# The mixer of a hybrid decoder as chains of steps in one list that fixes TensorE's order, with the substitution on GpSimd

## The chip, the core and the metric

The kernel runs on one core of a Trainium2 chip. A core has five engines with queues of their own, each of which works in order: TensorE (PE in the rows; PEld is its weight load), VectorE (DVE), ScalarE (ACT), GpSimd (POOL) and SyncE (SP), which issues the transfers. They wait for each other by semaphores. Matmul results land in PSUM, which GpSimd doesn't reach in this kernel; everything else is in SBUF. The metric is the time of one execution on the device in microseconds (us).

## The reference

256 tokens of width 1024 with 16 learned tokens ahead (272 columns in the kernel) pass two layers. Each layer is a half-weighted SwiGLU, a mixer and a second half-weighted SwiGLU. The mixer projects once and splits the columns among three groups of heads:

```python
def hybrid_mixer(h, ...):
    proj = h @ w_in
    sb_q, sb_k, sb_v, dn_qkv, dn_z, dn_b, dn_a, s5_u = jnp.split(proj, ...)
    o_sb = rmsnorm(stick_breaking_attention(heads(sb_q), heads(sb_k), heads(sb_v)), sb_out_norm)
    o_dn = gated_deltanet(dn_qkv, dn_z, dn_b, dn_a, dn_conv_w, dn_a_log, dn_dt_bias, dn_out_norm)
    o_s5 = rmsnorm(s5_mixer(s5_u, ...), s5_out_norm)
    return jnp.concatenate([o_sb, o_dn, o_s5], axis=-1) @ w_out

# gated_deltanet: qkv = silu(causal conv of 4 taps); q, k = l2norm; beta = sigmoid(b); g = decay
# per chunk of 64: t_inv = inverse of (I + strictly lower (beta k) k^T * decay)
# u = t_inv (beta v), w = t_inv (beta k exp(g)); state is carried from chunk to chunk
# result: rmsnorm(o, out_norm) * silu(z)
# s5_mixer: complex diagonal scan over time, y = gelu(...), then y * sigmoid(y @ w_glu + b_glu)
# stick_breaking: w = exp(log_sigmoid(z) + sum of log_sigmoid(-z) over later keys), out = w v
```

## The kernel before

All activations lie transposed, features on the 128 partitions and the 272 tokens along the columns. Every float32 product of a large weight is made from three matmuls of split halves (`xh`, `xl` and `wh`, `wl`; `mm3`), so that one projection unit of 128 output features takes 8 blocks times 3, or 24 matmuls of 272 columns. For each unit `weights` brings 512 KB into `raw` by SyncE, ScalarE rounds it to `wh`, and VectorE (for some units GpSimd, by `ON_POOL`) subtracts to get `wl`.

A mixer has 18 units of the input projection: six for the convolved q, k, v of DeltaNet (`conv`), four for S5 (`s5u`), two each for z and the stick-breaking q, k and v. Then it has small work:

- `dn_gates`: the gates, the decay matrices `E`, the key norm (`pn`), the products `LT`.
- `dn_inverse`: the inverse of each chunk's triangle. Blocks of 8 by substitution (`TT8`, `t8`, lines L1003 to L1008, on VectorE: seven pairs of a product and a difference of 9 to 63 elements a partition, then one masked copy to blocks of 32 and a transpose by 32), then blocks of 32, 64 and 128 by pairs of products `px`, `py`.
- `dn_rest`: norm of q, the products, then the state from chunk to chunk (`pk`, `pvn`, `pS`, and `pkt`, `pvt2` for the last tokens); `dn_norm` and `dn_out` (`po`, transposes, times z).
- `s5`: input products `pinc`, states by complex rotations and scans on VectorE (`w`, `x`, `s5z`); `s5_outputs` (`pY`, gelu) and `glu` (`pglu`, 48 matmuls).
- `sb`: `scores` (`pz`), `weights` (sums over later keys into the same `pz`, then Exp), `outputs` (`pob`, norm by `pnb`).

After it, `w_out` is applied in parts: `S` (S5's rows), `Y` (the rest). A part is two units at a time, named by their first output block, 4, 6, 0, 2.

A scheduler of the framework sets the order on each engine from the code's order, dependencies, estimated costs and priorities. The code's order is the string `ORD`; the blocks in `high_priority` (`FIRST` 4000 for gates, inverse and rest, `SECOND` 1500 for the S5 output) are drawn ahead. `HORD` orders the steps of `sb`, `ZT` names the PSUM tag of each head's scores (each tag has two buffers). `phase` places the loads of ScalarE's function tables, five in a mixer, and a NoSync order (`order`) keeps functions behind their table.

## Time and profile before

| | us |
|---|---|
| median of 3 runs (lowest to highest) | 1192.27 (1189.04 to 1202.69) |
| the profiled execution, and its span | 1194.31, span 1192.5 |
| mean granted TensorE clock over the span | 0.972 |
| busy: PE | 1154.8 (97%) |
| busy: VectorE | 853.6 (72%) |
| busy: ScalarE | 614.1 (52%) |
| busy: GpSimd | 175.3 (15%) |

The share of busy time is a mean over stages with different limits. The two mixers lie at 232.9 to 384.8 us and 821.0 to 977.9 us of the span, measured from the norm's sum over all features (`pms`) to the second group of `po` transposes. The granted clock is given as a share of 2.4 GHz, so 0.50 is 1.2 GHz. A busy time of TensorE holds overlapping records: a matmul that stands in the pipeline behind another counts, and so does one that goes slowly.

### The profile page before, as it was taken

The page shows a single profiled execution, that of the slowest core. Times are in us where ns is not written, and L with a number is a line of the kernel's source. Part 1 is how long each engine was busy: PE and PEld are TensorE (multiplying, and loading weights), DVE is VectorE, ACT ScalarE, POOL GpSimd, SP SyncE. Part 2 cuts the span into 40 slices and gives each one's busy share as a digit, 9 for nine tenths or more (in the row PEclk, how much of TensorE's full clock was granted, in tenths as well). Part 3 has the DMA queues.
Part 4 walks back from the last instruction along what each step waited for, and adds up shares of the span by engine and source line. Part 5 has one row for each costly group of instructions (what it writes and reads, how often), then busy time and mean ns, then how long its engine had stood idle before and what let it go on. Part 6 is the DMA issues. An engine that isn't in the chain of part 4 may idle for free.

```text
span 1192.5 us, 23762 instructions
## 1 busy us (share of the span) xinstructions
PE 1154.8 (97%) x9544; PEld 1104.5 (93%) x9544; DVE 853.6 (72%) x1648; ACT 614.1 (52%) x981; POOL 175.3 (15%) x210
## 2 busy tenths in 40 slices
PE   8999999999998999999999999999999989999997
PEld 7999999998786999999999999999988969999985
DVE  7999986699636866555579998756994268666644
ACT  6455575564166654444455556645632566555533
POOL 6312100021010111110201112011210001111100
PEclk9999999999789999999999999999997599999999
DMA  5656545543201455555565555455431015666663
GB/s 182 179 175 180 166 135 160 167 125 108 71 19 54 142 175 177 168 176 171 177 187 177 169 173 172 132 175 156 124 112 33 27 45 185 181 188 191 187 191 117
DMA packets 196858, 173.74 MB, mean 146 GB/s; under 512 B 21300, under 2 KB 193004, under 8 KB 196748
## 3 DMA queue, kind: packets, MB, share of 16 engines
q1 hardware_dynamic: 196732, 172.22, 48.2%
q8 instruction: 75, 1.23, 0.4%
q14 instruction: 35, 0.29, 0.1%
q10 hardware_dynamic: 16, 0.00, 0.0%
HBM read 171.15 MB, written 1.05 MB: 144 GB/s over the span
## 4 chain that ended last, share of the span: by engine, by line
PE 84%; DVE 10%; ACT 3%; issue 1%; DMA 1%; SPq 0%; ACTq 0%; DVEq 0%
PE proj L146 17%; PE proj L145 17%; PE proj L144 17%; PE pd L146 5%; PE pd L145 5%; PE pd L144 5%; PE pd L493 5%; DVE wl L139 2%; PE pY L852 1%; DVE qkv L1346 1%; DVE xT L1437 1%; PE pY L850 1%; PE pl L887 1%; PE pm L783 1%; PE pz L1227 1%
## 5 line engine op out<-in xcount | busy, mean ns | idle before, releaser
L144 PE MATMUL proj<-xh,wh 128*128 128x272 f32 (+1 forms) x1840 | 521.1, 289 | 6.3 <-DVE sy L1435 2.8
L145 PE MATMUL proj<-xl,wh 128*128 128x272 f32 (+1 forms) x1840 | 518.4, 287 | 0.2 <-DVE xl L1296 0.2
L146 PE MATMUL proj<-xh,wl 128*128 128x272 f32 (+1 forms) x1840 | 492.8, 290 | 3.3 <-DVE wl L139 3.0
L136 ACT ACTIVATE wh<-raw 128x1024 fp32r<-128x1024 f32 (+1 forms) x324 | 338.2, 1044 | 292.8 <-PE proj L145 99.5
L139 DVE TENSOR_TENSOR wl<-raw,wh 128x1024 fp32r<-128x1024 f32 (+1 forms) x312 | 378.4, 1213 | 146.6 <-PE pd L146 60.9
L144 PEld LDWEIGHTS proj<-xh,wh 128*128 128x128 f32 x1840 | 345.4, 188 | 10.5 <-DVE sy L1435 4.1
L145 PEld LDWEIGHTS proj<-xl,wh 128*128 128x128 f32 x1840 | 345.2, 188 | 3.0 <-issue 1.5
L146 PEld LDWEIGHTS proj<-xh,wl 128*128 128x128 f32 x1840 | 328.8, 187 | 7.2 <-DVE wl L139 5.8
L144 PE MATMUL pd<-hh,wh 128*128 128x272 f32 x528 | 149.6, 288 | 0.0
L145 PE MATMUL pd<-hl,wh 128*128 128x272 f32 x528 | 149.3, 288 | 0.0
L435 POOL TENSOR_TENSOR hl<-h,hh 128x272 fp32r<-128x272 f32 (+1 forms) x88 | 81.1, 924 | 452.9 <-ACT hh L434 452.8
L146 PE MATMUL pd<-hh,wl 128*128 128x272 f32 x528 | 140.8, 288 | 0.2
L144 PEld LDWEIGHTS pd<-hh,wh 128*128 128x128 f32 x528 | 99.2, 188 | 0.2
L145 PEld LDWEIGHTS pd<-hl,wh 128*128 128x128 f32 x528 | 99.3, 188 | 0.1
L146 PEld LDWEIGHTS pd<-hh,wl 128*128 128x128 f32 x528 | 95.1, 188 | 1.0 <-DVE wl L139 0.9
L107 ACT ACTIVATE g<-g 128x272 f32<-128x272 f32 (+2 forms) x92 | 37.6, 415 | 68.9 <-DVE g L429 68.8
L433 DVE TENSOR_TENSOR h<-proj,g 128x272 f32<-128x272 f32 (+1 forms) x88 | 37.7, 433 | 32.9 <-PE proj L146 21.3
L434 ACT ACTIVATE hh<-h 128x272 fp32r<-128x272 f32 (+1 forms) x88 | 36.4, 419 | 47.1 <-DVE h L433 47.1
L429 DVE TENSOR_TENSOR g<-proj,R 128x272 f32<-128x272 f32 (+1 forms) x88 | 37.5, 430 | 17.8 <-PE proj L146 17.6
L139 POOL TENSOR_TENSOR wl<-raw,wh 128x1024 fp32r<-128x1024 f32 x12 | 30.7, 2557 | 110.5 <-ACT th L107 34.9
L431 DVE TENSOR_TENSOR g<-g,R 128x272 f32<-128x272 f32 (+1 forms) x88 | 37.7, 432 | 12.6 <-ACT g L107 12.3
L376 POOL TENSOR_TENSOR acc<-acc,sq 128x272 f32<-128x272 f32 (+1 forms) x20 | 22.7, 1134 | 91.4 <-ACT sq L370 90.5
(490 smaller groups left out, 1310.1 us busy)
## 6 DMA issues: line engine op xcount, KB each, us to landing
raw<-in_ffn_w_gate_dram SPq DMA_DIRECT2D x88, 512.0 KB, 3.6
raw<-in_ffn_w_up_dram SPq DMA_DIRECT2D x88, 512.0 KB, 3.6
raw<-in_ffn_w_down_dram SPq DMA_DIRECT2D x70, 512.0 KB, 3.5
raw<-in_w_in_dram SPq DMA_DIRECT2D x36, 512.0 KB, 4.4
raw<-in_ffn_w_down_dram SPq DMA_DIRECT2D x24, 384.0 KB, 3.0
raw<-in_w_out_dram SPq DMA_DIRECT2D x16, 512.0 KB, 3.5
raw<-in_s_w_glu_dram SPq DMA_DIRECT2D x4, 512.0 KB, 3.4
xin<-in_x_dram SPq DMA_DIRECT2D x4, 256.0 KB, 5.8
```

The lines of the kernel that those rows point to most:

```text
L107: i = self.nc.scalar.activation(out, in_, func, **k)
L136: nc.scalar.activation(h[:, :n], r[:, :n], AF.Copy)
L139: e.tensor_tensor(l[:, :n], r[:, :n], f32(h[:, :n]), op=ALU.subtract)
L144: mm(p, wh, xh, start=first, stop=False)
L145: mm(p, wh, xl, start=False, stop=False)
L146: mm(p, wl, xh, start=False, stop=last)
L429: V.tensor_tensor(g1, pg[j][:, :N], R, op=ALU.mult)
L431: V.tensor_tensor(g1, g1, R, op=ALU.mult)
L433: V.tensor_tensor(h, pu[j][:, :N], g1, op=ALU.mult)
L434: nc.scalar.activation(hh[:, f, :N], h, AF.Copy)
L435: G.tensor_tensor(hl[:, f, :N], h, f32(hh[:, f, :N]), op=ALU.subtract)
L493: PE.matmul(pd[i][e], x[:, f, ts], w[:, 0, e * 512:e * 512 + 512], start=f == 0 and w is h and x is hh, stop=f == NF - 1 and w is lo)
```

## The change

The parts of the mixer become generators, with a `yield` after each step. One string, `MIX`, names the steps of all parts and the projection units in the order in which they are to be issued: C, U, Q, K, V, Z and a number are a projection unit; g, i, r, a and x advance the gates, the inverse, the rest, stick-breaking and the GLU by one step; p, t and y and a number are the input products, states and outputs of one of S5's four groups; l is the SiLU of the convolved q and v; v the transposes of the attention's values; n the load of the table of exp and ln; m S5's norm; o `dn_norm` and `dn_out`; S a part of `w_out`. Then each matmul of TensorE in the mixer is ordered behind the one before it in the list, by a NoSync dependency. The other engines are still ordered by the scheduler; the priorities are gone.

Beside that, the substitution moves from VectorE to GpSimd; ScalarE copies S5's `pinc` out of PSUM, and the states are then made from SBUF with operations of 544 columns in place of some of 272; z gets its SiLU from Tanh (no table of its own), with the gain and a factor 1/2 in `dn_out`'s scale; the SiLU of q and v comes in one step; the key norm comes ahead of the decay matrices; all scores have the PSUM tag `c`; the two rows of `Y` change places.

```diff
-FIRST, SECOND, URGENT, THIRD = 4000, 1500, 0, 0
-SBP = 0
-ORD = "czsrqgbmn"
-WOUT = "SnY"
-OTAG, NTAG, ZT = "d", "c", "cccd"
-HORD = (0, 1, 4, 2, 5, 3, 8, 6, 7, 9)
 SA, SB = 1, 1
-CONV, UORD, ZK = (0, 1, 4, 5), (0, 1, 2, 3), 0
+MIX = "C2 C3 U0 g U1 g g U2 g g g U3 g Q0 p0 p1 Q1 t0 p2 p3 K0 i t1 K1 a a t2 C0 a a i C1 i t3 a a i C4 i a a i C5 l i " \
+      "y0 V0 i y1 V1 i y2 Z0 y3 Z1 v r r r r x r r x r n a r r r r a m S4 S6 o S0 S2"
...
+        for o in range(2):
+            p = self.psum("b", "pinc")
             for b in range(4):
...
+                PE.matmul(p[:, b * NCH:(b + 1) * NCH], self.W1[o][:, 4 * b + r, :], self.U[:, r, b, :], start=True, stop=True)
+            A.copy(self.S[r][:, o], p[:, :T].rearrange("p (b c) -> p b c", b=4))
...
+        w, x = tl("w"), tl("x")
+        V.tensor_tensor(w, z, bc(cs, 1, 2), op=ALU.mult)
+        V.tensor_tensor(x[:, 0], z[:, 1], sn, op=ALU.mult)
+        V.scalar_tensor_tensor(flat(x[:, 1]), flat(z[:, 0]), -1.0, flat(sn), op0=ALU.mult, op1=ALU.mult)
+        V.tensor_tensor(z, w, x, op=ALU.add)
+        for o in range(2):
+            V.tensor_tensor_scan(flat(z[:, o]), flat(dec), flat(z[:, o]), 0.0, op0=ALU.mult, op1=ALU.add)
...
+        w, x = tl("w"), tl("x")
+        V.tensor_tensor(w, z, bc(cs, 1, 2), op=ALU.mult)
+        V.tensor_tensor(x, z, bc(sn, 1, 2), op=ALU.mult)
+        G.memset(z[:, :, :, 0:1], 0.0)
+        V.tensor_tensor(z[:, 0, :, 1:], w[:, 0, :, :-1], x[:, 1, :, :-1], op=ALU.subtract)
+        V.tensor_tensor(z[:, 1, :, 1:], w[:, 1, :, :-1], x[:, 0, :, :-1], op=ALU.add)
...
+        self.kn, kb = tl([P, 2, TP], "kn"), tl([P, 2, TP], "kb")
+        for b in range(2):
+            k, sq = qkv[:, 2 + b, :], self.c288("sq")
+            A.activation(sq, k, AF.Square)
+            p = self.psum("c", "pn")
+            PE.matmul(p[:, :TP], self.bd64, sq, start=True, stop=True)
+            self.rsqrt(sq, p[:, :TP], bias=self.eps)
+            self.newton(sq, p[:, :TP], self.c288("knt"), 1, EPS)
+            V.tensor_tensor(self.kn[:, b, :], k, sq, op=ALU.mult)
+        yield
         self.E = tl([P, 8, P], "E")
...
         TT8, t8 = tl([P, 9, 8], "TT8"), tl([P, 9, 8], "t8")
-        V.tensor_copy(TT8, bc(self.id8, 1, 9))
+        G.tensor_copy(TT8, bc(self.id8, 1, 9))
         for j in range(7):
-            V.tensor_tensor(t8[:, :, j + 1:], Lb[:, :, j + 1:, j], TT8[:, :, j:j + 1].to_broadcast([P, 9, 7 - j]), op=ALU.mult)
-            V.tensor_tensor(TT8[:, :, j + 1:], TT8[:, :, j + 1:], t8[:, :, j + 1:], op=ALU.subtract)
+            G.tensor_tensor(t8[:, :, j + 1:], Lb[:, :, j + 1:, j], TT8[:, :, j:j + 1].to_broadcast([P, 9, 7 - j]), op=ALU.mult)
+            G.tensor_tensor(TT8[:, :, j + 1:], TT8[:, :, j + 1:], t8[:, :, j + 1:], op=ALU.subtract)
         TT32, T32 = t9("TT32"), t9("T32")
-        V.tensor_tensor(TT32.rearrange("p u (b i) -> p u b i", b=4), bc(TT8, 2, 4),
+        G.tensor_tensor(TT32.rearrange("p u (b i) -> p u b i", b=4), bc(TT8, 2, 4),
                         bc(self.m8c.rearrange("p (b i) -> p b i", b=4), 1, 9), op=ALU.mult)
         V.transpose(fl(T32), fl(TT32))
+        yield
         for k in range(2):
...
         def scores(h):
             hs, b = slice(64 * (h % 2), 64 * (h % 2) + 64), h // 2
-            pz = self.psum(ZT[h], "pz")
+            pz = psum("pz")
             PE.matmul(pz[:, 0:272], k[hs, b, 0:128], q[hs, b, 0:272], start=True, stop=False, **skip)
             PE.matmul(pz[:, 272:416], k[hs, b, 128:256], q[hs, b, 128:272], start=False, stop=True, **skip)
             for c0, n in ((0, P), (272, P), (416, 16)):
...
             A.activation(h, y, AF.Copy)
             V.tensor_tensor(self.xl[:, slot + b, :], y, f32(h), op=ALU.subtract)
-        for x in HORD:
-            (scores if x < 4 else weights if x < 8 else outputs)(x % 4)
+        for f, x in ((scores, 0), (scores, 1), (weights, 0), (scores, 2), (weights, 1), (scores, 3),
+                     (weights, 2), (weights, 3), (outputs, 0), (outputs, 1)):
+            f(x)
+            yield
...
+            def do_z(b):
+                proj(1536, zr, b)
+                t = self.cv("zt")[:, :T]
+                self.act(t, zr[:, b, :], AF.Tanh, scale=0.5)
+                V.scalar_tensor_tensor(zr[:, b, :], t, 1.0, zr[:, b, :], op0=ALU.add, op1=ALU.mult)
+            def silu():
                 self.phase(SET_SILU)
-                for b in range(2):
-                    self.act(zr[:, b, :], zr[:, b, :], AF.Silu)
-                    V.tensor_scalar(zr[:, b, :], zr[:, b, :], self.dng[:, l], None, op0=ALU.mult)
-            def do_s5():
...
-            for x in WOUT:
-                if x == "n":
-                    with first():
-                        self.dn_out(zr, 2)
-                    continue
-                if x == WOUT[-1]:
-                    self.norm_begin(*nxt)
-                for d0 in (4, 6, 0, 2):
-                    w_out_part(x, d0, "ab"[d0 // 2 % 2])
-                    if x == WOUT[-1]:
-                        for d in {4: (4, 5), 6: (6, 7), 0: (), 2: (0, 1, 2, 3)}[d0]:
-                            self.norm_block(d, d0 == 2, t0)
...
+            chains = dict(g=self.dn_gates(l, qkv, ba), i=self.dn_inverse(), r=self.dn_rest(qkv),
+                          a=self.sb(l, q, k, v, 0), x=self.glu(l, u))
+            steps = dict(C=conv, U=s5_in, Q=lambda b: proj(0, q, b), K=lambda b: proj(256, k, b), V=lambda b: proj(512, v, b),
+                         Z=do_z, p=lambda r: self.s5_inputs(u, r), t=self.s5_states, y=lambda r: self.s5_outputs(u, r),
+                         l=silu, v=lambda: self.sb_values(), n=norms, S=lambda d0: w_out_part("S", d0, "ab"[d0 // 2 % 2]),
+                         o=lambda: (self.dn_norm(), self.dn_out(zr, self.dng[:, l], 2)),
+                         m=lambda: self.rms(self.acc, 4 * 512, 0, self.R5, "b"))
+            done = len(nc.cur_bb.bb.instructions)
+            for x in MIX.split():
+                if x in chains:
+                    next(chains[x], None)
+                else:
+                    steps[x[0]](*(int(n) for n in x[1:]))
+            assert all(next(c, 0) == 0 for c in chains.values())
+            pe = [i for i in nc.cur_bb.bb.instructions[done:] if i.engine == mybir.EngineType.PE]
+            for i, j in zip(pe, pe[1:]):
+                self.order(j, i)
+            self.norm_begin(*nxt)
+            for d0 in (4, 6, 0, 2):
+                w_out_part("Y", d0, "ab"[d0 // 2 % 2])
+                for d in {4: (4, 5), 6: (6, 7), 0: (), 2: (0, 1, 2, 3)}[d0]:
+                    self.norm_block(d, d0 == 2, t0)
             self.blocks = (4, 0)
```

Three places show how the order moves. The first is TensorE's queue in layer 0 at the key norm, where `pn` sums the squares `sq` of one block of k. Before:

```order
1733 L144 MATMUL proj<-xh,wh 128x272
1734 L959 MATMUL pn<-sq,bd_384 128x288
1735 L963 MATMUL pbeta<-ba,sel_575 128x288
1736 L145 MATMUL proj<-xl,wh 128x272
1737 L146 MATMUL proj<-xh,wl 128x272 x2
...
1755 L145 MATMUL proj<-xl,wh 128x272
1756 L959 MATMUL pn<-sq,bd_384 128x288
1757 L146 MATMUL proj<-xh,wl 128x272
```

After:

```order
1681 L143 MATMUL proj<-xh,wl 128x272
1682 L926 MATMUL pn<-sq,bd_385 128x288 x2
1683 L939 LDWEIGHTS identb
1684 L939 MATMUL pdc<-negl,identb 128x512
1685 L941 MATMUL pdc<-triI,gs 128x128 x4
1686 L141 MATMUL proj<-xh,wh 128x272
```

Before, the two `pn` stand twenty rows apart, with projections and other products between them; after, they stand side by side ahead of the decay matrix `pdc`.

The second is VectorE's queue in layer 0 at the substitution, the operations on `t` and `TT` (`s5z` are S5's states). Before:

```order
483 L1005 TENSOR_TENSOR t_3313<-Lb,TT_3312 128x9x7
484 L835 TENSOR_TENSOR w<-s5z_3954,cs 128x544
485 L836 TENSOR_TENSOR x<-s5z_3954,sn 128x544
486 L1006 TENSOR_TENSOR TT_3312<-TT_3312,t_3313 128x9x7
487 L1364 SCALAR_TENSOR_TENSOR pq<-proj,R 128x272
488 L139 TENSOR_TENSOR wl<-raw,wh 128x1024
489 L838 TENSOR_TENSOR s5z_3954<-w,x 128x4x67
490 L839 TENSOR_TENSOR s5z_3954<-w,x 128x4x67
491 L1005 TENSOR_TENSOR t_3313<-Lb,TT_3312 128x9x6
492 L825 TENSOR_TENSOR w<-pinc,cs 128x272
```

After, where `T` is the transpose that ends the substitution, and `L1260` belongs to the stick-breaking weights:

```order
476 L824 TENSOR_TENSOR w<-s5z_3458,cs 128x544
477 L825 TENSOR_TENSOR x<-s5z_3458,sn 128x272
478 L826 SCALAR_TENSOR_TENSOR x<-s5z_3458,sn 128x272
479 L827 TENSOR_TENSOR s5z_3458<-w,x 128x544
480 L1387 SCALAR_TENSOR_TENSOR pk<-proj,R 128x272
481 L136 TENSOR_TENSOR wl<-raw,wh 128x1024
482 L829 SCALAR_TENSOR_TENSOR s5z_3458<-dec,s5z_3458 128x272 x2
483 L832 TENSOR_TENSOR w<-s5z_3458,cs 128x544
484 L833 TENSOR_TENSOR x<-s5z_3458,sn 128x544
485 L1260 SCALAR_TENSOR_TENSOR W_588<-pz,W_588 128x432
486 L1014 STREAM_TRANSPOSE T_3644<-TT_3643 128x288
487 L1260 SCALAR_TENSOR_TENSOR W_588<-pz,W_588 128x432
```

And GpSimd's queue after, ahead of that transpose:

```order
47 L136 TENSOR_TENSOR wl<-raw,wh 128x1024
48 L834 MEMSET s5z_3457 128x8
49 L1009 TENSOR_TENSOR t_3627<-Lb,TT_3626 128x9x7
50 L1010 TENSOR_TENSOR TT_3626<-TT_3626,t_3627 128x9x7
51 L1009 TENSOR_TENSOR t_3627<-Lb,TT_3626 128x9x6
```

The pairs of the substitution stood between the operations of the S5 states in one queue; now GpSimd makes them, and VectorE's transpose has its place behind those of the third state.

The third is TensorE's queue in layer 0 at the first norm of the attention's output. Before:

```order
2286 L1251 MATMUL pob<-W_586 64x272
2287 L1252 MATMUL pob<-W_586,W_587 64x144
2288 L1253 MATMUL pob<-W_586,vt 64x16
2289 L1242 MATMUL pz<-W_587,nsufI 128x432
2290 L1243 MATMUL pz<-W_587,nones 128x144
2291 L1244 MATMUL pz<-W_587,nones 128x2x16
2292 L1257 MATMUL pnb<-sbr,bd_384 128x272
```

After:

```order
2229 L1275 MATMUL pob<-W_587 64x272
2230 L1276 MATMUL pob<-W_587,W_588 64x144
2231 L1277 MATMUL pob<-W_587,vt 64x16
2232 L1281 MATMUL pnb<-sbr,bd_385 128x272
2233 L1159 MATMUL pS<-qkv,kg 64x64 x4
2234 L1161 MATMUL pS<-qkv,E 128x64 x4
2235 L1176 MATMUL pkt<-qkv,kn 32x64
```

And ScalarE's queue after, up to the square `sbr` that `pnb` reads:

```order
271 L104 ACTIVATE th<-pglu,prm 128x272
272 L1323 ACTIVATE xh<-s5u,prm 128x272 x3
273 L1328 ACTIVATE gsq<-s5u 128x272
274 L133 ACTIVATE wh<-raw 128x1024
275 L104 ACTIVATE th<-pglu,prm 128x272
276 L94 ACT_TABLE_LOAD
277 L1155 COPY qkv<-pvn 128x256
278 L1323 ACTIVATE xh<-s5u,prm 128x272
279 L1328 ACTIVATE gsq<-s5u 128x272
280 L1279 ACTIVATE sbr<-pob 128x272
```

Before, three matmuls of another head's weights stand between `pob` and `pnb`; after, `pnb` follows `pob` at once and the state's update `pS` stands behind it, while ScalarE has the GLU's operations, a weight and a table load ahead of `sbr`.

## Rows read from the trace of the kernel before

**Rows 1.** Windows: us, length, busy PE, PEld, DVE, ACT, POOL, then clock, DMA share, GB/s.

```profile
232.90:304.80 71.90, 70.02 (x549) 65.96 (x547) 68.23 (x140) 39.28 (x65) 13.03 (x12) 1.00 0.41 118
304.80:324.60 19.80, 17.43 (x284) 14.12 (x288) 12.37 (x27) 2.19 (x5) 0.11 (x1) 0.57 0.18 55
...
341.70:348.50 6.80, 5.96 (x31) 5.77 (x30) 1.92 (x5) 2.85 (x9) 0.73 (x1) 0.50 0.00 0
348.50:384.80 36.30, 32.31 (x248) 25.60 (x247) 22.55 (x51) 25.39 (x51) 3.05 (x2) 1.00 0.19 59
...
500.00:600.00 100.00, 100.00 (x801) 100.00 (x800) 55.86 (x68) 46.24 (x62) 14.13 (x15) 1.00 0.57 174
821.00:892.90 71.90, 70.03 (x550) 65.99 (x548) 68.26 (x140) 39.32 (x65) 13.02 (x12) 1.00 0.41 118
892.90:911.70 18.80, 16.34 (x314) 12.81 (x318) 11.98 (x27) 2.55 (x6) 0.11 (x1) 0.64 0.19 58
...
925.40:949.30 23.90, 23.47 (x120) 22.30 (x119) 4.91 (x15) 9.72 (x23) 2.35 (x1) 0.50 0.07 23
949.30:977.90 28.60, 24.66 (x188) 18.89 (x187) 18.16 (x42) 20.65 (x41) 0.29 (x1) 1.00 0.17 56
```

**Rows 2.** Windows of the tile `proj` alone: length, busy PE, PEld, DVE, then clock.

```profile
232.90:304.80 71.90, 57.93 (x409) 52.79 (x407) 8.50 (x18) 1.00 0.41 118
```

**Rows 3.** ScalarE's groups by form, 232.9 to 384.8: count, busy us, mean ns, idle.

```profile
L136 ACT ACTIVATE wh<-raw 128x1024 fp32r<-128x1024 f32 x22 | 23.2, 1056 | 24.9 <-PE proj L145 24.7
L97 ACT ACT_TABLE_LOAD x5 | 6.4, 1283 | 0.1
...
L107 ACT ACTIVATE W<-W 128x432 f32<-128x432 f32 x8 | 4.2, 556 | 0.0
L107 ACT ACTIVATE W<-pz 128x432 f32<-128x432 f32 x8 | 4.1, 530 | 5.7 <-PE pz L1244 3.4 <-PE pz L1231 2.2
...
L1295 ACT ACTIVATE xh<-s5u,prm 128x272 fp32r<-128x272 f32 x4 | 2.9, 761 | 0.0
L107 ACT ACTIVATE qkv<-qkv 128x272 f32<-128x272 f32 x6 | 2.4, 417 | 1.8 <-DVE qkv L1346 1.8
L1300 ACT ACTIVATE gsq<-s5u 128x272 f32<-128x272 f32 x3 | 2.0, 678 | 0.7 <-DVE s5u L1292 0.7
L107 ACT ACTIVATE th<-pglu,prm 128x272 f32<-128x272 f32 x4 | 1.9, 476 | 0.6 <-PE pglu L146 0.6
```

**Rows 4.** GpSimd's `Lm` group, then timelines at 264 and 286: start, us, operation.

```profile
L1001 POOL TENSOR_TENSOR Lm<-L,lev 128x288 f32<-128x288 f32 x2 | 2.1, 1044 | 6.7 <-ACT qkv L1344 6.7
...
264.24 0.50 DVE L1346 SCALAR_TENSOR_TENSOR qkv<-pad,prm,qkv 128x272 f32<-128x272 f32 x1
...
264.86 1.00 PE L821 MATMUL pinc<-s5U,W 128*128 128x68 f32 x8
264.91 2.37 POOL L139 TENSOR_TENSOR wl<-raw,wh 128x1024 fp32r<-128x1024 f32 x1 [3.25 <-PE proj L146]
265.17 2.95 DVE L1346 SCALAR_TENSOR_TENSOR qkv<-pad,prm,qkv 128x272 f32<-128x272 f32 x2
...
286.55 3.10 POOL L139 TENSOR_TENSOR wl<-raw,wh 128x1024 fp32r<-128x1024 f32 x1 [1.42 <-PE proj L146]
```

**Rows 5.** VectorE's groups by form, 232.9 to 384.8: count, busy us, mean ns, idle.

```profile
L139 DVE TENSOR_TENSOR wl<-raw,wh 128x1024 fp32r<-128x1024 f32 x17 | 20.7, 1216 | 5.5 <-PE proj L146 5.0 <-issue 0.6
...
L832 DVE TENSOR_TENSOR_SCAN s5z<-dec,s5z 128x272 f32<-128x272 f32 x8 | 5.3, 704 | 0.0
...
L835 DVE TENSOR_TENSOR w<-s5z,cs 128x544 f32<-128x544 f32 x4 | 2.9, 718 | 0.0
...
L121 DVE SCALAR_TENSOR_TENSOR sby<-pnb,sbr 128x272 f32<-128x272 f32 x2 | 0.9, 441 | 0.0
```

**Rows 6.** Timeline of one head's scores on TensorE: start, us, first and last form.

```profile
371.60 0.72 PE L1227 MATMUL pz<-pq,pk 64*128 64x272 f32 x2
...
372.73 0.21 PE L1231 MATMUL pz<-pq,pk 64*16 64x16 f32 x2
```

More of the change, by code (lines that the diff above doesn't have):

```diff
@@ new lines, in s5_outputs @@
+    def s5_outputs(self, u, r):
+        PE = self.nc.tensor
+        p = self.psum("b", "pY")
+        for b in range(4):
+            q = 4 * b + r
+            po = p[:, b * NCH:(b + 1) * NCH]
+            PE.matmul(po, self.M0[:, q, :], self.U[:, r, b, :], start=True, stop=False)
+            for k in range(2):
+                PE.matmul(po, self.W2[k][:, q].rearrange("p k g c -> p (k g c)"), self.S[r][:, k, b], start=False, stop=k == 1)
+        for t in range(4):
+            o = u[32 * r:32 * r + 32, :, t * NCH:t * NCH + NCH]
+            self.act(o, p[32 * t:32 * t + 32, :T].rearrange("p (b c) -> p b c", b=4), AF.Gelu_apprx_tanh)
@@ L1183, in dn_norm, with dn_out @@
         V.tensor_tensor(o, o, bc(r, 2, 64), op=ALU.mult)
-    def dn_out(self, zg, slot):
+    def dn_out(self, zg, g, slot):
         nc = self.nc
@@ L1212, in sb, with values @@
         vt = [t.rearrange("p (h d) -> p h d", d=64) for t in (wf[:, 1728:1984], ef[:, 1728:1984], tmp.tile([P, 256], F32, name="vt"))]
-        for c, (t0, n) in enumerate(TOK):
-            pv = psum("pvs")
-            for b in range(2):
-                PE.transpose(pv[:n, b * P:b * P + P], v[:, b, t0:t0 + n], self.ident)
-            A.copy(vt[c][:n], pv[:n, :256].rearrange("p (h d) -> p h d", d=64))
+        def values():
+            for c, (t0, n) in enumerate(TOK):
+                pv = psum("pvs")
+                for b in range(2):
+                    PE.transpose(pv[:n, b * P:b * P + P], v[:, b, t0:t0 + n], self.ident)
+                A.copy(vt[c][:n], pv[:n, :256].rearrange("p (h d) -> p h d", d=64))
+        self.sb_values = values
         W = [wf[:, h * 432:h * 432 + 432] for h in range(4)]
@@ L1247, in outputs @@
         def outputs(b):
-            po = self.psum(OTAG, "pob")
+            po = self.psum("d", "pob")
             for h in (2 * b, 2 * b + 1):
@@ L1321, in mixer @@
         t0 = NMETA if l == DEPTH - 1 else 0
-        first = lambda: self.tc.high_priority(FIRST)
-        second = lambda: self.tc.high_priority(SECOND)
         self.norm_end()
@@ L1358, in mixer @@
                 V.tensor_tensor(u[:, b, :].rearrange("p (j c) -> p c j", j=4), i(p[:, :T]), i(R), op=ALU.mult)
-            zr = tmp.tile([P, 2, T], F32, name="pz")
-            def proj(c0, dst):
-                for b in range(2):
-                    p, = self.unit(w_in[:, c0 + b * P:c0 + b * P + P], P)
-                    V.scalar_tensor_tensor(dst[:, b, :], p[:, :T], 0.125 if c0 == 0 else 1.0, R, op0=ALU.mult, op1=ALU.mult)
-            q, k, v = (tmp.tile([P, 2, T], F32, name=f"p{n}") for n in "qkv")
@@ L1368, in do_z @@
-            def do_z():
-                proj(1536, zr)
-                self.phase(SET_SILU)
-                for b in range(2):
-                    self.act(zr[:, b, :], zr[:, b, :], AF.Silu)
-                    V.tensor_scalar(zr[:, b, :], zr[:, b, :], self.dng[:, l], None, op0=ALU.mult)
-            def do_s5():
-                with self.tc.high_priority(THIRD):
-                    self.s5(u)
-            def do_rest():
-                with first():
-                    self.dn_rest(qkv)
@@ L1404, in do_norm, with proj @@
-            def do_norm():
-                with first():
-                    self.dn_norm()
-            def do_r5():
-                with second():
-                    self.rms(self.acc, 4 * 512, 0, self.R5, "b")
-            steps = dict(z=do_z, s=do_s5, r=do_rest, q=do_qkv, b=do_sb, c=do_conv, g=do_glu, n=do_norm, m=do_r5)
-            for x in ORD:
-                steps[x]()
-            rows = dict(S=((4, 5, 6, 7),), B=((0, 1),), D=((2, 3),), X=((0, 1), (2, 3)), Y=((2, 3), (0, 1)))
+            def proj(c0, dst, b):
+                p, = self.unit(w_in[:, c0 + b * P:c0 + b * P + P], P)
+                V.scalar_tensor_tensor(dst[:, b, :], p[:, :T], 0.125 if c0 == 0 else 1.0, R, op0=ALU.mult, op1=ALU.mult)
@@ new lines, in do_z, with norms @@
+            def do_z(b):
[4 more added lines that the diff above has]
+            def silu():
+                self.phase(SET_SILU)
+                for b in (0, 4):
+                    self.act(qkv[:, b:b + 2, :T], qkv[:, b:b + 2, :T], AF.Silu)
+                self.phase(SET_GELU)
+            def norms():
+                self.phase(SET_LNEXP)
@@ L1419, in w_out_part @@
+            rows = dict(S=((4, 5, 6, 7),), Y=((0, 1), (2, 3)))
             def w_out_part(x, d0, tag):
```

140 lines of the change are left out of this document (51 added, 89 removed).

## The prediction

> **What bounds the kernel now.** I read the profile's first page, then the windows by stage through both mixers, then the groups of each engine inside them, and last the timeline where GpSimd works beside VectorE. The profiled execution took 1194.31 us (span 1192.5), against a median of 1192.27, so 2 us are to be taken off when a sum is brought to the median's scale. TensorE is busy for 97% of the span, so time can only come from three places, and the windows show where these are [rows 1]. Outside the mixers 801 projection matmuls stand in 100 us, 0.125 us each, without a gap: nothing is to be had there, and the order of TensorE is nearly the same there in both kernels.
>
> A mixer, from the norm's sum to the second `po` transposes, takes 151.9 us in layer 0 and 156.9 in layer 1. Its first 71.9 us hold nearly all projections; TensorE's records cover 70 us of it, but VectorE's cover 68.2. The 407 projection matmuls [rows 2] are worth 50.9 us at 0.125, and the other 140 or so about 15.5 (some 0.11 each, near the eight `pinc` in one microsecond [rows 4]): 66.4, so that 5.5 us per mixer are waiting that the overlapping records hide. Then the projections run out. From 304.8 and 892.9 on the rest of DeltaNet, the GLU and stick-breaking go by with idle time and at the lower clock.
>
> What a perfect order could win is the sum of three. Idle time, window length less busy time, the first stretch included: 1.9+2.4+0.8+4.0 = 9.1 us in layer 0 and 1.9+2.5+0.4+3.9 = 8.7 in layer 1 [rows 1] (the stretches not shown, 324.6 to 341.7 and 911.7 to 925.4, have none). Half clock, busy time times one less the granted clock: 17.43x0.43+5.96x0.5 = 10.5 and 16.34x0.36+23.47x0.5 = 17.6, an upper bound, since a short matmul need not take half the time at twice the clock. Hidden waiting: 2x5.5 = 11. Together 17.8+28.1+11 = 57 us.
>
> **The change part by part.** The matmuls are the same in number and shape. The list gives their order, and no matmul may now overtake one that waits. I walked that order by hand with the durations of the rows, and added up what TensorE would wait in one mixer.
>
> (a) Key norm. The two `pn` stand side by side, where before sixteen and more projections lay between them. The second needs ScalarE to finish, in this order, a SiLU 0.42, the table load 1.28, exp, ln and exp of about 0.2 to 0.5 each, and a square 0.43: 3.5 us after the square of the first, which itself comes a `wh` (1.06) and a SiLU after the unit [rows 3]. Part of that head lies beside the unit: 4.5 us, between 2 and 5.5.
>
> (b) Substitution. The copy, fourteen small operations and the masked one go to GpSimd. VectorE is rid of them in the stretch where it is the bound, which is worth at most a part of the 11 us counted above. GpSimd takes some 3.7 us for the fourteen (0.2 us and 2 ns an element, between its 32-element copies and its 1024-element `wl`) and 1.05 for the masked one, the `Lm` row [rows 4]. With the copies ahead and the transpose behind this is a chain of 8.4 us, and TensorE has work for 11 between `pl8` and `px`: two projection units of 3 us, three scores of 1.3 [rows 6], and weights 1.2. So the chain alone is covered. VectorE's queue is not: the transpose that ends the chain stands there behind two whole S5 states of 6.0 us each (four operations of 544 columns at 0.71, two scans at 0.70, four of 272 at 0.43), 5.1 us of a third, two `wl` of 1.2, three evictions of 0.43 and some 0.6 for the 432 columns of `W`: 22 us with the transpose itself [rows 5]. VectorE starts on them about 2.6 us behind `p1` on TensorE, which has 19 us of work from there (Q1 3, `p2` and `p3` 2, K0 3, and the 11). That is 5.5 us late; records of VectorE overlap by some 0.07 us each, 2 us on this count. I take 4, between 0 and 9.
>
> Here lies the danger. While GpSimd ran `wl` for 2.37 us, two VectorE operations with two tensor inputs took 2.95 us together, where one takes 0.50 free, and GpSimd's own `wl` took 3.10 us beside others [rows 4]. So the two engines hold each other up. The Trainium skill states this as a rule against such a move (GPSIMD Engine Reference, 1. Specifications and 8. Key points): GpSimd shares its SBUF interfaces with VectorE and contends with its instructions of two SBUF inputs, and VectorE is about twice as fast elementwise. By that rule the 4.8 us of GpSimd would add to VectorE's queue whole, some 9 us over both mixers; the rows show it for long operations, and none shows it for short ones.
>
> (c) All `pz` share two buffers, where one of four had another tag. Scores 2 and 3 wait for the Exp of the weights, 0.53 behind two operations of 0.56 [rows 3]: 0.85+1.85 = 2.7 us, between 1 and 4.
>
> (d) `py2` stands behind a SiLU table load and the SiLU of two blocks on ScalarE, and C5 hides most: 1.2 us.
>
> (e) The tail, `v r r r r x r r x r n a r r r r a m`. No projection is left there; 48 GLU matmuls, 6 us, are the only cover, while before put two `w_out` units and late scores between the same steps. TensorE waits at the first `pn` 2.6 (`wh` and five operations of 0.4 on ScalarE, less the transposes); at `pl` and `pv` 0.8; at `pk` 0.5; at the first `pnb` 4.75 (th, three xh, gsq, wh, th, the table load, a copy, xh, gsq and the square are 8.5 us on ScalarE [rows 3], of which half a GLU part, `pvn` and `pob`, 3.2 us, lie beside it, and overlap takes the rest); at `pkt` 2.65 (three Newton steps of 0.44 [rows 5] stand ahead of the four updates of the state); at the two `pvt2` 2.15; at the second `pnb` 0.65. Sum 14.1, between 9 and 18.
>
> (f) Clock. Through the middle the inverse now lies between projections, and I expect full clock there. The tail keeps some 8 us of small work among waits; at 1.2 GHz that is 8 us more. Before, one such stretch ran at 1.00 (348.5 to 384.8) and another at 0.50 (925.4 to 949.3) [rows 1]: I take half, 4, between 0 and 10.
>
> (g) At nothing: eight more `pinc` copies on ScalarE (3.4 us of an engine busy for 52%, behind K and Q units), Tanh for SiLU on z, the gain in `dn_out`'s scale, the S5 states from SBUF (VectorE's count per state stays 6 us). Cover gone, the copies would cost their 0.43 each, 3.4 per mixer.
>
> Sum per mixer 4.5+4+2.7+1.2+14.1+4 = 30.5, for two 61, against the 57 that fall away: 4 us slower, 1198.5 on the profile's scale and about 1197 on the median's. What the weave wins in the inverse it gives back at the key norm and in the tail.
>
> **The rivals.** *The weave wins.* My waits are added as if each stood alone, but a wait gives ScalarE and VectorE time to catch up, and what follows waits less. Were half of (a), (c) and (e) so absorbed, 10.6 us per mixer, and the clock kept, 4 more as (f) falls to 0, the time is 1197-29 = 1168; with half of that, 1182. Middle 1174. For it: before's own tail carries most of these steps with 4.0 us idle in 36.3 at full clock [rows 1]. Against it: it had projections among them.
>
> *Slower: GpSimd and VectorE block each other.* One mechanism at one place: if each of the fourteen short GpSimd operations must wait out the VectorE operation under way (up to 0.72, an S5 product [rows 5]), the chain grows by up to 10 us to 18.4, and VectorE's queue by up to the 4.8 of GpSimd. It decides once the two reach `px` more than 4 us late (beyond the term taken). Then `px` waits 9 to 11 instead of 4 and the idle engine drops to half clock over `px`, `pz` and `py`, about 4 us of small work: 10 per mixer, 1197+20 = 1217.
>
> *It doesn't do what it says.* The list fixes only TensorE's order; if the DeltaNet chain from the gates to `po` has the same length in both, 150 us, the mixer ends where it ended, at 1192.
>
> **How the numbers follow.** One per cent, 12 us, is about what a measurement of this kernel can tell from no change: the three runs before lie between 1189 and 1203. Chances: forecast 1197 0.24 and the unchanged chain at 1192 0.12, both within 1%; the weave wins 0.31; slower 0.33, the blocking for 0.2 of it, and the upper ends of (a), (e) and (f) together (1.0+3.9+6 per mixer, 1219) for the rest. Faster by over 1% 0.31, within 1% 0.36, slower by over 1% 0.33. The range goes from the fully absorbed waits, 1168, to the blocking with some more of the tail, 1221; it is as wide as the two unknowns, (b) and (e), make it, and since cases of both signs hold most of the chance, the likeliest one's own range is 1184 to 1205.
>
> **What would show each step.** Right: a wait of TensorE's second `pn` on ScalarE's `sq` of 3 us or more; `px` on VectorE's transpose, with VectorE rather than GpSimd busy before it; `pnb` on `sbr` of 4 us or more; full clock from the norm to `pY`; the mixers near 155 us. Wrong: mixers under 145 us with short waits in the tail (the weave wins), or over 162 with GpSimd's short operations at 0.5 us and more (the blocking). Most would be wrong if the projections between the steps lie so that ScalarE is always ahead, or if the half clock of before returns in the middle.

## The result and the profile after

The changed kernel takes 1230.59 us (median of 4 runs, 1227.27 to 1235.31) against 1192.22 for the one before: a ratio of 1.031, 95% interval 1.024 to 1.038. It is slower by 38 us and lies outside the predicted range of 1168 to 1221. Its profiled span is 1228.3 us.

The loss is in the mixers alone. From the norm's sum to the second `po` they last 174.9 and 174.1 us, against the 151.9 and 156.9 of before, 40 us more in all; the stretches outside together are some 4 us shorter. The windows of the kernel after show the first mixer whole, then each of its stretches at half clock, and at the end the second mixer (columns as in [rows 1]):

```profile
231.60:406.50 174.90, 153.43 (x1414) 138.62 (x1414) 109.96 (x215) 81.37 (x153) 26.57 (x35) 0.83 0.22 62
244.80:251.70 6.90, 3.60 (x14) 2.69 (x13) 4.28 (x11) 4.06 (x9) 0.27 (x3) 0.51 0.29 78
258.50:261.90 3.40, 3.40 (x17) 3.40 (x16) 0.25 (x1) 0.00 (x0) 0.00 (x0) 0.50 0.39 118
268.70:272.20 3.50, 3.50 (x18) 3.50 (x17) 3.25 (x8) 0.81 (x2) 1.80 (x2) 0.51 0.02 5
299.50:306.30 6.80, 6.18 (x95) 5.33 (x95) 6.80 (x14) 3.00 (x6) 0.00 (x0) 0.50 0.30 80
333.60:340.40 6.80, 6.80 (x33) 6.80 (x33) 0.00 (x0) 1.55 (x4) 0.00 (x0) 0.50 0.17 60
357.50:371.10 13.60, 12.99 (x77) 12.06 (x77) 3.80 (x10) 1.54 (x3) 0.00 (x0) 0.50 0.07 25
384.80:401.90 17.10, 13.73 (x81) 9.91 (x80) 9.30 (x26) 5.12 (x13) 0.29 (x1) 0.50 0.00 1
840.50:1014.60 174.10, 152.92 (x1415) 138.00 (x1414) 109.10 (x214) 81.21 (x153) 24.77 (x34) 0.83 0.21 61
```

The reader is to take two numbers from this. Idle time of TensorE, length less busy time, is 174.9-153.4 = 21.5 us in layer 0 and 21.2 in layer 1, against 9.1 and 8.7 before [rows 1]. And the clock falls to 1.2 GHz seven times in a mixer, for 58 us in all, where before it fell twice in each, for some 24 us in layer 0 and 37 in layer 1 [rows 1]. The matmuls that lie in these seven stretches are worth 50.2 us of busy time, half of which, 25 us, is lost to the clock at most; by the same count [rows 1] lost 10.5 and 17.6. So 12.4 us of idle time and 14.6 us of clock are added in layer 0, 12.5 and 7.4 in layer 1 (whose clock of 0.83 gives the same 25); what remains of the mixers is 4 and 2.7 us shorter. Where the waits stand is told by TensorE's waits in the first mixer of the kernel after (total, times, longest):

```profile
PE pn L926 <- ACT sq L924: 5.2, 2, 3.3
PE pnb L1281 <- ACT sbr L1279: 3.7, 2, 3.2
PE plt L886 <- DVE LT L883: 3.4, 1, 3.4
PE pz L1266 <- DVE W L1260: 2.2, 1, 2.2
PE pkt L1176 <- DVE qkv L1170: 1.8, 1, 1.8
PE pvs L1238 <- ACT W L1239: 1.4, 1, 1.4
```

The first line is the key norm. The timeline of TensorE there shows what a wait sets off:

```profile
242.16 0.29 PE L143 MATMUL proj<-xh,wl 128*128 128x272 f32 x1
244.31 0.84 PE L926 MATMUL pn<-sq,bd 128*128 128x288 f32 x2 [1.86 <-ACT sq L924]
248.45 1.33 PE L926 MATMUL pn<-sq,bd 128*128 128x288 f32 x2 [3.30 <-ACT sq L924]
249.57 0.63 PE L939 MATMUL pdc<-negl,identb 128*128 128x512 bf16 x1
250.00 1.86 PE L941 MATMUL pdc<-triI,gs 128*128 128x128 f32 x8
```

Each `pn` is one sum, recorded as two matmuls (x2). Between 242.4 and 248.4 TensorE has only the first of them to do, with a wait of 1.86 us ahead of it and one of 3.30 behind. At 244.8 the clock falls, and stays down until 251.7, so that the second `pn` (1.33 us against 0.84 for the first) and the decay matrix behind it run at half speed.

### The profile page after: what moved, and what is told of

The parts are those of the page before. It is cut to its first block, busy times and chain, and to the rows that moved or that the text cites. A ratio compares the mean times of both kernels' runs of the same rounds, so it can differ in the third digit from the quotient of the medians.

```text
span 1228.3 us, 23740 instructions
## 1 busy us (share of the span) xinstructions
PE 1167.8 (95%) x9544; PEld 1118.5 (91%) x9544; DVE 857.5 (70%) x1609; ACT 623.2 (51%) x993; POOL 190.1 (15%) x242
## 4 chain that ended last, share of the span: by engine, by line
PE 84%; DVE 10%; ACT 4%; issue 2%; DMA 1%; SPq 0%; ACTq 0%; DVEq 0%
PE proj L143 17%; PE proj L141 17%; PE proj L142 17%; PE pd L143 5%; PE pd L142 5%; PE pd L141 5%; PE pd L490 5%; DVE wl L136 2%; PE pY L847 1%; DVE qkv L1372 1%; PE pY L845 1%; DVE s5z L829 1%; PE pm L780 1%; DVE x L833 1%; PE pz L1266 1%
## 5 line engine op out<-in xcount | busy, mean ns | idle before, releaser
L141 PE MATMUL proj<-xh,wh 128*128 128x272 f32 (+1 forms) x1840 | 530.6, 294 | 0.6 <-DVE sy L1424 0.6
L142 PE MATMUL proj<-xl,wh 128*128 128x272 f32 (+1 forms) x1840 | 525.9, 291 | 0.2
L143 PE MATMUL proj<-xh,wl 128*128 128x272 f32 (+1 forms) x1840 | 497.9, 293 | 2.0 <-DVE wl L136 1.8
L141 PEld LDWEIGHTS proj<-xh,wh 128*128 128x128 f32 x1840 | 354.2, 193 | 3.2 <-issue 1.6
L142 PEld LDWEIGHTS proj<-xl,wh 128*128 128x128 f32 x1840 | 353.4, 192 | 1.6 <-DVE xl L362 0.6
L143 PEld LDWEIGHTS proj<-xh,wl 128*128 128x128 f32 x1840 | 336.1, 191 | 4.7 <-DVE wl L136 3.5
L428 DVE TENSOR_TENSOR g<-g,R 128x272 f32<-128x272 f32 (+1 forms) x88 | 37.8, 433 | 12.4 <-ACT g L104 12.1
```

The costliest lines, as they stand in the source:

```text
L141: mm(p, wh, xh, start=first, stop=False)
L142: mm(p, wh, xl, start=False, stop=False)
L143: mm(p, wl, xh, start=False, stop=last)
L428: V.tensor_tensor(g1, g1, R, op=ALU.mult)
```

## The experiments

Times are medians; before was measured anew in each group of runs, at 1190.2 to 1191.6 us.

| run | us | ratio to before, 95% interval |
|---|---|---|
| changed kernel | 1230.6 | 1.031 [1.024, 1.038] |
| e1_fill | 1222.7 | 1.027 [1.025, 1.029] |
| e2_sub_vector | 1246.2 | 1.047 [1.045, 1.048] |
| e3_before_pool | 1194.5 | 1.003 [0.996, 1.010] |
| e4_nopin | 1172.5 | 0.985 [0.983, 0.987] |
| e5_list | 1245.4 | 1.044 [1.040, 1.049] |
| e6_nopin_vector | 1180.5 | 0.990 [0.985, 0.994] |
| e7_nopin_list | 1174.6 | 0.985 [0.980, 0.991] |
| e8_pin_front | 1207.6 | 1.013 [1.009, 1.017] |
| e9_nopin_prio | 1172.0 | 0.985 [0.983, 0.987] |
| e10_nopin_tail | 1174.8 | 0.987 [0.984, 0.990] |
| e11_pin_sched | 1174.6 | 0.987 [0.984, 0.989] |
| e12_split_norm | 1218.9 | 1.024 [1.020, 1.027] |

**Is it the fixed order at all?**

```diff
-            for i, j in zip(pe, pe[1:]):
-                self.order(j, i)
```

> The changed kernel without the dependencies that fix TensorE's order: the list still sets the order of issue, but the scheduler may let matmuls overtake. If the fixing is the loss (a ready matmul behind one that waits): 1195 to 1215, with TensorE's idle time per mixer down from 21 to under 14 us. If the list's sequence itself and the lost priorities are the loss: 1220 to 1245.

It took 1172.5 us: 58 us less than the changed kernel, below the expected band, and 1.5% faster than the kernel before. The windows of both mixers of this run:

```profile
231.70:377.50 145.80, 138.05 (x1422) 123.74 (x1422) 110.93 (x216) 81.45 (x154) 28.75 (x35) 0.96 0.27 81
811.10:955.90 144.80, 136.82 (x1422) 122.89 (x1421) 110.75 (x215) 81.14 (x154) 26.95 (x34) 0.97 0.27 81
```

Idle time is 7.8 and 8.0 us, and the granted clock of 0.96 and 0.97 leaves some 12 and 9 us at half clock (twice 0.04 of 145.8, twice 0.03 of 144.8). All other parts of the change are in this run, so all of them together are a gain of 18 us, and the fixed order loses three times as much. The timeline of its TensorE at the first `pn` shows how: the sum comes as a visitor between projection matmuls, and its wait is passed while they run.

```profile
248.01 0.29 PE L142 MATMUL proj<-xl,wh 128*128 128x272 f32 x1
248.14 0.65 PE L926 MATMUL pn<-sq,bd 128*128 128x288 f32 x2
248.41 0.51 PE L143 MATMUL proj<-xh,wl 128*128 128x272 f32 x1
...
255.85 0.29 PE L141 MATMUL proj<-xh,wh 128*128 128x272 f32 x1
255.98 0.65 PE L926 MATMUL pn<-sq,bd 128*128 128x288 f32 x2
```

**Is it the fixing, or the sequence that is fixed?**

```diff
+SCHED = {...}   # rank of each matmul in the order of e4_nopin
+            pe.sort(key=lambda i: SCHED[i.name])
             for i, j in zip(pe, pe[1:]):
                 self.order(j, i)
```

> TensorE's order in the mixer fixed as in the changed kernel, but by a table that holds, matmul by matmul, the order that the scheduler chose in the run without the fixed order (1172). If the sequence is what costs and not the fixing: 1168 to 1178, the waits of that run again. If fixing costs by itself (the added dependencies, the scheduler's choices on the other engines): above 1185.

1174.6 us, with mixers of 147.8 and 148.6 us, in which TensorE's records follow each other in the same order as in e4_nopin. An order that is fixed costs nothing that these runs can tell when it is the order that the scheduler chose matmul by matmul. The list's sequence is the loss. The scheduler also orders the other engines anew for each order of TensorE; how much of the loss comes through their queues was not separated.

**Front or tail of the list?** Here the fixing ends at the step `v`.

```diff
+                if x == "v":
+                    cut = len(nc.cur_bb.bb.instructions)
-            pe = [i for i in nc.cur_bb.bb.instructions[done:] if i.engine == mybir.EngineType.PE]
+            pe = [i for i in nc.cur_bb.bb.instructions[done:cut] if i.engine == mybir.EngineType.PE]
```

> The changed kernel with the order fixed only up to the transposes of the values (the step v); the tail is free. If the losses of front and tail add up, as the windows say (of 29 us per mixer against the run without the fixed order 18 lie ahead of v and 11 behind it): the free tail gives 20 to 24 us, 1204 to 1212. If a late front makes the tail late anyway: less than 10 us, above 1220.

1207.6 us: the free tail returns 23 us, as added up, and the other 35 us belong to the front. Its windows show a mixer of 164.8 us at 233.8, with 16.2 us idle.

**Is it the clock?** The waits were filled with work that nobody needs:

```diff
+    def fill(self, n):
+        p = self.psum("a", "fill")
+        for _ in range(n):
+            self.nc.tensor.matmul(p[:, :256], self.ident, self.M0[:, 0:2].rearrange("p q i -> p (q i)"), start=True, stop=True)
...
+            self.fill(8 if b else 4)
             PE.matmul(p[:, :TP], self.bd64, sq, start=True, stop=True)
```

and in the same way 6 ahead of `plt`, 4 of the first weights, 2 of the last `pvs`, 6 and 1 of the two `pnb`, 3 of `pkt`.

> The changed kernel with 34 spare matmuls of 256 columns per mixer put ahead of the matmuls that wait longest (both key-norm sums, the last product of the key, the first head's weights, the last transposes of the values, the attention's norm, the last tokens' product); they write a PSUM buffer that nobody reads and add about 18 us of work per mixer, at most as long as the waits in front of which they stand. Theory 1 (the clock: each wait of a few us is followed by a stretch at 1.2 GHz, and this costs 25 us per mixer, more than the 21 us of waiting): the half-clock stretches behind the filled waits go, their sum falls from 58 us per mixer to under 35, and the time falls to 1205 to 1222 although work was added. Theory 2 (the waits alone are the loss, and the clock falls anyway because the small products of the mixer are thin): the half-clock time stays above 50 us per mixer and the time stays at 1225 to 1240.

1222.7 us, 8 us faster with 68 more matmuls: just above the band of the clock theory (1205 to 1222) and below the other's. The windows of this run show its first mixer and the stretches at half clock in it, and the last line the filler alone (length, busy PE, PEld, then clock):

```profile
232.70:402.50 169.80, 161.17 (x1482) 144.99 (x1482) 106.98 (x210) 80.87 (x153) 26.46 (x35) 0.90 0.21 64
258.90:262.30 3.40, 3.40 (x17) 3.40 (x16) 0.00 (x0) 0.00 (x0) 0.00 (x0) 0.50 0.08 24
299.90:306.70 6.80, 6.09 (x93) 5.37 (x94) 6.80 (x13) 2.61 (x6) 0.10 (x1) 0.50 0.28 80
334.00:340.80 6.80, 6.80 (x33) 6.80 (x32) 0.00 (x0) 1.56 (x4) 0.00 (x0) 0.50 0.15 53
357.90:371.50 13.60, 12.99 (x77) 12.06 (x77) 3.80 (x10) 1.55 (x3) 0.00 (x0) 0.50 0.07 24
391.90:395.30 3.40, 3.40 (x11) 2.27 (x12) 0.93 (x2) 0.79 (x2) 0.12 (x1) 0.52 0.00 0
...
232.70:402.50 169.80, 16.87 (x68) 12.60 (x68) 0.90 0.21 64
```

Idle time falls from 21.5 to 8.6 us because the filler takes its place, so the waits themselves were not shortened by this. The clock, 0.83 before filling, is 0.90: 169.8x0.10x2 = 34 us at half clock instead of 58. The stretches between and behind the two `pn` and behind `plt` are gone, and the one behind the attention's norm is down from 17.1 to 3.4 us. The four others stay: 258.9 to 262.3, a projection unit behind the second decay matrix, and three (from 299.9, 334.0 and 357.9) where scores, `pY` and the small products of DeltaNet lie close together. The five stretches hold 32.7 us of busy time against 50.2, so that at most 8.8 us less are lost to the clock; the filler's 16.9 us are 4.0 more than the 12.9 of idle time that went. The difference, 4.8, is near the 5.1 us by which the mixer is shorter. So the waits bring on part of the half clock. That thin work brings on the rest is not tested by a run, but idle time in the records is not needed for it: in the kernel after 6.80 of 6.80 us are busy at 0.50 (333.6 to 340.4), and before 23.47 of 23.9 (925.4 to 949.3 in [rows 1]).

**One wait repaired.** The two `pn` become separate steps with U2 between them.

```diff
-MIX = "C2 C3 U0 g U1 g g U2 g g g U3 g ...
+MIX = "C2 C3 U0 g U1 g U2 g g g g g U3 g ...
...
             V.tensor_tensor(self.kn[:, b, :], k, sq, op=ALU.mult)
-        yield
+            yield
```

> The changed kernel with one repair in its fixed order: the two sums of the key norm are separate steps, and the unit U2 stands between them, where it stood two steps later. If a wait costs what it lasts and the half clock behind it as well: the wait of 3.3 us goes and so does a good part of the 6.9 us at half clock that begin in it (3 us of lost work), 5 to 6 us per mixer and 8 to 13 us in all, 1218 to 1223. If the list only moves waits about (U2 is missing as cover between the two decay matrices, and the next wait comes sooner): within 4 us of the changed kernel, 1226 to 1235.

1218.9 us, 11.7 us less than the changed kernel. The first mixer of this run, and the window that held 3.60 us of work at half clock:

```profile
231.40:398.40 167.00, 148.46 (x1415) 134.04 (x1414) 108.72 (x215) 81.14 (x153) 26.58 (x35) 0.87 0.22 64
244.80:251.70 6.90, 6.53 (x51) 5.91 (x49) 4.37 (x10) 5.84 (x12) 0.12 (x2) 1.00 0.28 78
```

The second `pn` waits 0.37 us instead of 3.30. In layer 0 the mixer is 167.0 us long, 7.9 us less for a wait of 3 us: idle time is 3.0 us less (18.5), and the rest is clock (0.87 instead of 0.83). But this is the execution of 1213.2 us, the fastest of seven, whose others took 1218.4 to 1220.4; by the medians the repair gave 5.8 us per mixer. That a wait costs itself and about as much again was thus measured on one wait. That the second half lies directly behind it is not shown: in this execution half clock went from 244.8, but also from 258.5 and from 3.4 us of the tail, where no wait was repaired.

**Repair of the whole list by hand.** Besides the split norm, projection units were moved ahead of the waits seen, z's units went to the tail, two parts of `w_out` went between the tail's last steps, and the chains g, i and r got priority 4000 on the other engines. Z1 there reads the shared input after the GLU's first step has overwritten part of it, so what this run and e7_nopin_list leave in z isn't the reference's; their work is the same in size.

```diff
+MIX = "C2 C3 U0 g U1 U2 g Q0 g g g g K0 g U3 g Q1 p0 p1 K1 t0 p2 p3 C0 i t1 a a C1 a a i t2 C4 i a a t3 i C5 i a a l i V0 i " \
+      "y0 V1 i y1 i y2 y3 v r Z0 r r r x r r x r Z1 n a r m S4 r r S6 r a o S0 S2"
...
-        yield
+            yield
...
-                    next(chains[x], None)
+                    with self.tc.high_priority(4000 if x in "gir" else 0):
+                        next(chains[x], None)
```

> TensorE's order fixed as in the changed kernel, but by another list: the two key-norm sums are separate steps with a projection unit ahead of each, the products of the key and the first states have a unit between, z's units and two parts of the S5 output projection stand in the tail, and the gates, inverse and rest have priority 4000 on the other engines. If the loss lies in where this list puts the waits (repairable): idle per mixer falls from 21 to under 13 us, half clock from 58 to under 35, and the time to 1180 to 1205. If any fixed order loses (a wait that the list did not foresee blocks everything behind it): above 1210.

1245.4 us: the repair made it worse, by 15 us. List and priority changed together here, so which of the two did it is not shown. The time is in the band of "any fixed order loses", which e11_pin_sched refutes in this form: what lost are the orders that I wrote by hand. The longest waits seen before are gone or shorter, and others stand in their places; the first mixer of this run is 182.0 us long, with 22.9 us idle and a clock of 0.82. TensorE's longest waits in it:

```profile
PE po L1215 <- DVE qkv L1203: 4.0, 1, 4.0
PE plt L886 <- DVE LT L883: 2.7, 1, 2.7
PE pz L1251 <- ACT W L104: 2.1, 2, 1.5
PE px L1021 <- DVE T L1014: 1.9, 1, 1.9
PE pdc L941 <- DVE gs L937: 1.7, 1, 1.7
```

The same list, free, and without the priority:

> The other list of the run before the last, without the fixed order and without the priority. If the list's sequence still matters when the scheduler may reorder: different from 1172 by more than 6 us, and I expect faster, 1160 to 1168. If the scheduler decides alone: 1166 to 1178.

1174.6 us, 71 less than with the order fixed, and not distinguishable from 1172.5, where I expected it to be faster: neither list matters much once TensorE's order is the scheduler's. Two more edits of the free kernel say the same. S5's norm and two parts of `w_out` were named earlier in the tail (`n a r m S4 r r S6 r a o S0 S2`), and the steps g, i and r were wrapped in `high_priority(4000)`:

> Without the fixed order, and with S5's norm and the first two parts of the output projection named earlier in the list's tail, between the last steps of DeltaNet's rest. If the scheduler's order follows its own estimates: within 6 us of 1172. If the list's sequence helps it: 1160 to 1166, with less idle time and no half clock behind the attention's norm.

> Without the fixed order, and with priority 4000 on the steps of the gates, the inverse and the rest, as the kernel before had it on the same parts. If the lost priorities cost the changed kernel something: faster than 1172 by 5 us or more. If the order of issue does their work: within 5 us of 1172; if drawing the chain ahead starves the projections: slower, 1178 to 1190.

1174.8 and 1172.0 us: neither moves the time. With e4_nopin, the last is the fastest version found.

**The substitution.** It was put back on VectorE in the changed kernel, put back in the free one, and moved alone in the kernel before (each time `V.` for `G.`, or the reverse, in the copy, the pairs and the masked operation).

> The changed kernel with the substitution back on VectorE; everything else stays. Theory of the blocking engines (short GpSimd operations of 0.2 us took 0.3 to 1.1 us beside VectorE's S5 products, and this holds up TensorE): faster than the changed kernel by 10 us or more, under 1220. Theory 1 (waits elsewhere and the clock): TensorE's px did not wait for the substitution at all, so the time stays within 1% of the changed kernel, 1218 to 1242; since VectorE gets 5 us more per mixer, rather on the slow side.

> The changed kernel without the fixed order and with the substitution back on VectorE. The run without the fixed order took 1172. If GpSimd's part of the gain is real: slower than that by 5 us or more, 1178 to 1192, near the kernel before. If the move mattered only where the order was fixed (TensorE then waited 9.7 us for the transpose of the substitution): within 1% of 1172, 1165 to 1178.

> The kernel before with the substitution alone moved to GpSimd, in the scheduler's own order. If the move costs by itself (blocking): slower than before by 5 us or more, 1197 to 1210. If it is neutral or a small gain (VectorE's bound stretch gets shorter): 1180 to 1195. In either case far from the changed kernel's 1230, since theory 1 puts the loss on the fixed order.

1246.2, 1180.5 and 1194.5 us. Back on VectorE it costs 15.6 us with the fixed order, above both bands expected, because TensorE then does wait for VectorE's queue, as the first line of its waits shows:

```profile
PE px L1021 <- DVE T L1014: 9.7, 1, 9.7
```

and 8 us with the free one. There TensorE's idle time is less than with GpSimd (4.5 and 5.8 us in the two mixers against 7.8 and 8.0), and the clock is lower (0.91 and 0.89 against 0.96 and 0.97); by what way the substitution brings that on is not shown. In the kernel before, the move alone changes nothing that can be told: its four runs took 1185.8, 1186.2, 1202.7 and 1203.2 us. In the profiled one, of 1202.7, one mixer is longer than before (167.1 us, at a clock of 0.85) and one shorter (148.5, at 0.94); why is not shown. The blocking theory falls: in the changed kernel, with either order, the move is a gain.

## Why the prediction was wrong

**The step that failed is (f), the clock.** It said "Through the middle the inverse now lies between projections, and I expect full clock there", and put 4 us per mixer. The clock falls five times ahead of the tail, among projection units of 3 us, and 25 us per mixer are lost to it: 11.7 in the middle, where (f) had nothing, and 13.4 in the tail, where it had 4 and at most 10. Predicted for both mixers: 8 us; measured: 50. The 28.1 us of half clock before were right as a count, but the change did not take them away, it nearly doubled them. The prediction's last sentence names half clock in the middle among what would make most of it wrong; its only price was some 4 us around `px` in the blocking rival. The place to see it was in [rows 1]: the clock of before fell where waits and short products met (304.8 to 324.6), and with hardly a wait behind short products that lie close together (925.4 to 949.3, behind `px` and `pY`); the fixed order brings such places in between the projections. The Trainium skill tells of a like pattern for waits on transfers (TensorE: Matmul & The Clock Gate, HAM oscillation — how this bites in real kernels): a matmul kernel that waits at each step goes back to the lower clock at each. Here the waits are for other engines, and five of the seven windows agree: they begin in or right behind a listed wait. The two from 258.5 and 333.6 begin behind short products, with no listed wait just ahead.

**The waits were sized well in sum and not in place.** Predicted 26.5 us of waiting per mixer, measured 21.5 of idle time. (a) 4.5, measured 5.2: right, in place and cause. (b) 4 at `px`, measured 0 there: the transpose came at 298.95, and TensorE was held until 298.2 by another victim of the same queue, the weights' `pz`, 2.2 us, and had scores to do until `px` at 302.4. Not foreseen was `plt`, 3.4 us: VectorE had six `s5U` copies ahead of `LT`. The rows of both:

```profile
298.24 0.99 PE L1266 MATMUL pz<-W,nsufI 128*128 128x432 f32 x2 [2.18 <-DVE W L1260]
298.95 0.48 DVE L1014 STREAM_TRANSPOSE T<-TT 128x288 f32<-128x288 f32 x1 [0.76 <-POOL s5z L834]
302.45 1.18 PE L1021 MATMUL px<-T,Lm 32*32 32x32 f32 x72
...
263.71 3.53 DVE L809 COPY s5U<-s5u 32x272 f32<-32x272 f32 x6
267.28 0.69 DVE L883 TENSOR_TENSOR LT<-pl,E 128x512 f32<-128x512 f32 x1
```

(c) 2.7, measured 1.2. (d) 1.2, measured none. (e) 14.1, measured 9.4 in the listed waits of the tail (1.4 at `pvs`, 0.5 each at `pn` and `pv`, 0.4 at `pk`, 3.7, 1.8, and 1.1 at `pvt`). That is a third less than the term; whether ScalarE and VectorE caught up while TensorE waited, as the first rival said, was not separated. That the sum came near is in part luck: 5.6 us that no term had, at `plt` and at the weights' `pz`, stand against what (b) to (e) had too much. The 11 us of hidden waiting were mis-sized: 71.9-66.4 = 5.5 holds the 1.9 us of idle time that the idle sum counts too. Without it 3.6 per mixer stay, or 7.2, and the remainder of the mixers is 6.7 us shorter.

So the sum was 57 that fall away against 61 that come. With the hidden waiting put right it would have been some 53 against 61, 8 us slower instead of 4. With the measured terms: idle 17.8, clock 28.1 and 6.7 of the hidden make 52.6 that fall away, against idle 42.7 and clock 50 that come, 92.7: 40 us for the mixers. That this is what was measured says nothing more, since the 6.7 is the remainder. Of the 36 us by which the sum is off, the clock is 42 too little, the waits 10 too much, and what falls away 4 too much.

**The rivals.** That the weave wins was wrong for this list; e4_nopin has the time that this rival gave (1168 to 1182), but by another way, since there no order is fixed. The blocking of GpSimd and VectorE is there and does not decide. Its sign in the prediction, mixers over 162 us with GpSimd's short operations at 0.5 us and more, did come, for half of those operations; it is e2_sub_vector and e6_nopin_vector that show that the blocking is not the cause. The short operations that I put at 0.2 to 0.33 us took up to 1.12 beside VectorE, as the timeline of GpSimd in the kernel after shows:

```profile
289.74 0.34 POOL L1009 TENSOR_TENSOR t<-Lb,TT 128x63 f32<-128x63 f32 x1
...
293.91 1.12 POOL L1009 TENSOR_TENSOR t<-Lb,TT 128x27 f32<-128x27 f32 x1
295.11 0.55 POOL L1010 TENSOR_TENSOR TT<-TT,t 128x27 f32<-128x27 f32 x1
...
297.17 0.58 POOL L1009 TENSOR_TENSOR t<-Lb,TT 128x9 f32<-128x9 f32 x1
297.83 0.22 POOL L1010 TENSOR_TENSOR TT<-TT,t 128x9 f32<-128x9 f32 x1
298.13 0.79 POOL L1012 TENSOR_TENSOR TT<-TT,m8c 128x288 f32<-128x288 f32 x1
```

The fifteen operations take 8.1 us, and 9.2 with the gaps between them, where I put 4.8. The Trainium skill states that GpSimd shares its SBUF interfaces with VectorE and contends with its instructions of two SBUF inputs (GPSIMD Engine Reference, 8. Key points). That fits: the operation of 1.12 us lies beside a `wl` of VectorE with two such inputs. To leave the substitution on VectorE for it would still have been wrong here, by 15.6 us with the fixed order, where the same work waits its turn in a queue that TensorE follows, and by 8 us with the free one. "It doesn't do what it says" is refuted by e4_nopin and e11_pin_sched: TensorE's order is worth 58 us, or 56 by e11_pin_sched.

**What I did not ask** is the question that the free order answers: which matmul would stand in the place of the one that waits. I added up the list's waits against those of the scheduler, but took each as a loss of its own length, and gave what follows a wait a price only in the tail, the 4 us of (f), and around `px` in the blocking rival.

What stays open: how much of e4_nopin's gain of 18 us over the kernel before comes from which of the smaller edits. GpSimd's part is 8 us by e6_nopin_vector; the list as code order, the `pinc` copies, Tanh for SiLU, the one SiLU step and the remaining small edits share the other 10, and were not taken apart.
